# The low-part product of attention scores over 128 rows in place of 64

## The chip, the cores and the metric

One core of one Trainium2 chip. The metric is the device time of one execution in microseconds (us), the median of several runs. TensorE (PE) multiplies; its weight loads are listed apart as PEld. VectorE is DVE, ScalarE is ACT, GpSimd is POOL. SyncE (SP) issues nearly all DMAs, in the order of its queue.

## What is computed

Two layers of a decoder trunk over 1024 tokens of width 1024, in fp32. Layer 0 mixes tokens by two groups of attention heads behind one projection; layer 1 by a state-space recurrence and a short convolution. Each layer then has an MLP of width 4096 and a gated embedding. The change lies in layer 0's attention. Of the reference, the scores that it touches:

```python
sc = jnp.einsum('bqhcd,bkhcd->bhcqk', q_blk, kf) * scale      # dense heads, head width 64
sc = jnp.where(kpos[None, :] <= qpos[:, None], sc, -jnp.inf)
a = jax.nn.softmax(sc, axis=-1)
w = a[:, :, 0] - lam * a[:, :, 1]
```

The second group (a mixture of dilated windows) is computed as one masked softmax too, over the same kind of scores with another table of masks.

## The kernel before

**Exact operands in two parts.** An fp32 operand is split into a high part of type fp32r (`hi`, line 75, on ACT) and the low rest (`lo`, line 78, on DVE); a product is three matmuls, high by high, high by low and low by high (`mm3`, lines 93 to 95).

**The stage.** `attention` runs `at_start` and then `at_run`. `at_start` loads the eight blocks of x (line 1057), splits them, and makes q and k of pair 0. `at_run` goes through eight pairs of heads; a pair has two maps c = 0, 1 of head width 64, and the 1024 queries are taken in eight blocks of 128 (`qb`), two to a step. The score tile of one block has (qb + 1) x 128 columns, in pieces of at most 512.

**A score tile** (`emit_s`, line 1454) is two matmuls into one PSUM bank S of three. The contraction of a head is 64 long, so the tile of k that is read has k's high part in one half of the partitions and k's low part in the other, and the tile of q has q's high part twice. Line 1470 multiplies those over 128 rows: high by high plus high by low. Line 1471 adds q's low part by k's high part, over the 64 rows that hold them:

```python
nc.tensor.matmul(S, qk["q"][c][:, q], qk["k"][c][:, k], start=True, stop=False)
nc.tensor.matmul(S, qk["ql"][me, q], qk["k"][c][me, k], start=False, stop=True)
```

Then DVE adds the mask and takes the row minimum (line 1473), ACT takes the exponential (line 1478), and for the first four pairs DVE combines two maps (line 1492). Weights are transposed (line 1503), split, and multiplied with v (`pvu`, lines 93 to 95, 1527 and 1528).

**q and k** (`qk_out`, line 1154) are made half by half, 512 tokens each: DVE scales (`z`), ACT gives the high part (`zh`), DVE the low part. The pieces go to their places by DMAs of 64 rows on SP's queue (lines 1176 and 1177): four for a half of k, four for a half of q. q's low part needs no DMA, DVE writes it straight to the tile `ql`. `z`, `zh` and `zl` are tiles of one tag `z` of four buffers, which `ple_proj` (`ppo`) and `out_a` (`sq2`) use too. The tags `q0`, `q1`, `ql`, `k0`, `k1` have two buffers each, 1024 tokens wide; `at_start` borrows q's and k's for the blocks of x, and `ple_proj` for its operand.

**Order.** PE's order is set while the program is built: `at_run` weaves scores, transposes, products with v and filler (projections of the next pairs) by a model of costs. The other engines' orders come from the scheduler, SP's among them.

Of the kernel before, what the change touches and what calls it, by code (L numbers as in the profile page):

```python
# [7 lines left out]
F32 = mybir.dt.float32  # L8
F32R = mybir.dt.float32r
# [8 lines left out]
P = 128  # L18
T = 1024          # tokens
H = 512           # tokens of one matmul  # L20
D = 1024
KB = D // P       # 128-row blocks of the model width
FB = 32           # 128-row blocks of the MLP width
# [4 lines left out]
class Weave:  # L28
    """Order of TensorE's work: lanes of items that may start at a time, and filler for the waits."""
# [35 lines left out]
class Trunk:  # L65
# [40 lines left out]

    def rstd_split(self, acc, pool, width, tags, tags2=("z", "z", 4), bank=None):
        """(sum over partitions of acc / n_mean + eps) ** -0.5 on every partition, by the function returned."""
# [11 lines left out]
    def rstd_sum(self, accs, pool, width, tags, bank=None):  # L120
        """As rstd_split, of a sum of accs."""
        def sums(ps):
            for a in accs:
                self.nc.tensor.matmul(ps, self.ones.bitcast(F32), a, start=a is accs[0], stop=a is accs[-1])
        return self.rstd_of(sums, pool, width, tags, bank or self.bank)
# [22 lines left out]
    def xsplit(self, h, g, xp):  # L148
        """hi and lo of g * h, g per partition."""
# [74 lines left out]
    def chains(self, jobs, kbs):  # L224
        """jobs: (weights, operands, columns of the weights per block, half); the contraction outermost."""
# [12 lines left out]
    def blocks(self, src, xs, count, kbs, out, lead=2, split=None, pre=()):  # L238
        """Blocks m of W^T x: out(m, half, psum). The first ones take the contraction, or its two parts, outermost."""
# [24 lines left out]
    def stats_new(self, acc, sq):  # L264
        """Sums of squares; acc and sq are the (pool, tag, bufs) of their tiles."""
        return {"acc": None, "at": acc, "sq": sq}
# [11 lines left out]
    def rstd_full(self, st, rp, pool, n_z=4):  # L278
        """Inverse root mean square of each token, on every partition."""
# [91 lines left out]
    def ple(self, l, xs, st0, tp, xp):  # L371
# [3 lines left out]
        def out(m, n, ps):  # L375
# [13 lines left out]
            # tokens from (chunk, t) to (t, chunk)  # L389
# [10 lines left out]
    def ple_last(self, xs, st0, tp, wp):  # L400
# [4 lines left out]
        def final(hn, acc, s, n):  # L405
# [8 lines left out]
            if end:  # L414
                # with the gains applied before; few and large stores
# [69 lines left out]
    def pexp(self, out, x, tmp):  # L485
        """exp(x), to the last bits, 0 below the normal numbers."""
# [18 lines left out]
    def sincos(self, so, co, x, tmp):  # L505
# [18 lines left out]
        # the quadrant  # L524
# [22 lines left out]
    def s5_prep(self):  # L547
        """Matrices of the recurrence over chunks of 8 tokens, four groups at a time, to DRAM."""
# [3 lines left out]
        with tc.tile_pool(name="prep", bufs=1, side=LEFT, reuse_waits="tile") as pr:  # L552
# [23 lines left out]
            # powers 0..8 of the transition, and 7..0  # L576
# [22 lines left out]
            # (a - 1) / lambda  # L599
# [15 lines left out]
            # decay and rotation of one chunk  # L615
# [24 lines left out]
    def spill(self, pr, q, j, full):  # L640
        """hi and lo of a [128, 512] operand to DRAM."""
# [8 lines left out]
    def s5_quad(self, q, pr, pw, rv, cr, ci, rot, sgn, nsgn):  # L650
# [22 lines left out]
        def outer(out, tab, nt, X1, X2):  # L673
            """out[s, g, t, c] = tab0[s, t, g] X1[s, g, c] + tab1[s, t, g] X2[s, g, c]"""
# [15 lines left out]
        # rotation tables  # L690
# [42 lines left out]
    def recurrent(self, xp):  # L733
        tc, nc, A = self.tc, self.nc, self.A
        with tc.tile_pool(name="rc", bufs=1, side=RIGHT, reuse_waits="tile") as self.ap:
            gs, w = self.rc_run(xp)
            # the gate of the recurrence
# [19 lines left out]
    def rc_run(self, xp):  # L757
# [14 lines left out]
        # u, tokens on partitions, for two sets of 16 groups  # L772
# [52 lines left out]
        def conv(cb):  # L825
            """A block of channels of the gated convolution; tokens are (t, chunk)."""
# [26 lines left out]
            # the tokens before t = 0 are those of the chunk before  # L853
# [38 lines left out]
        def g_tiles(k):  # L892
            """Half of a block of the gate's operand, in the place of a quad's matrices."""
# [5 lines left out]
        def quad(q):  # L899
# [17 lines left out]
            def f_s():  # L917
# [16 lines left out]
                # back from the rotating frame, one chunk later  # L934
# [14 lines left out]
            def f_y():  # L949
# [4 lines left out]
                # by hi and lo of the matrices next to each other, summed on the way out  # L954
# [78 lines left out]
    def at_start(self, xp):  # L1033
        """hi and lo of the gained x, the first q and k as they come, and the inverse root mean squares."""
# [15 lines left out]
        for k in range(KB):  # L1050
            x = ap.tile([P, T], F32, name="x", tag=("q0", "q1", "k0", "k1")[k % 4], bufs=2)
# [47 lines left out]
    def ple_proj(self, l, m0, m1):  # L1099
        """(w_ple_proj^T p^T) of one layer, blocks m0 to m1, to DRAM; yields after each 128-row block of the contraction."""  # L1100
# [4 lines left out]
        for k in range(2):  # L1105
            raw = self.wp.tile([P, T], F32, tag="wr", bufs=2, name="praw")
            nc.sync.dma_start(raw, A["pT"][l, k])
            h, lo = [ap.tile([P, T], F32R, tag=t + str(k), bufs=2, name="ph") for t in "qk"]
            self.hi(h, raw)
            self.lo(lo, raw, h)  # L1110
            ps.append((h, lo))
        yield 0.0
        for m in ms:
# [3 lines left out]
            for n in range(2):  # L1117
                s = slice(n * H, (n + 1) * H)
                b = self.bank()
                for k in range(2):  # L1120
                    c = slice(k * 512 + (m % 4) * P, k * 512 + (m % 4) * P + P)
                    self.mm3(b, (ww[0][:, c], ww[1][:, c]), (ps[k][0][:, s], ps[k][1][:, s]), k == 0, k == 1)
# [30 lines left out]
    # projections: generators that yield after each 128-row block of a contraction  # L1153
    def qk_out(self, i, which, n, ps):
        nc, ap = self.nc, self.ap
        d = self.qkt.setdefault(i, {})
        if which not in d:
            d[which] = [ap.tile([P, T], F32R, name=f"{which}{c}", tag=f"{which}{c}", bufs=2) for c in range(2)]
            if which == "q":
                d["ql"] = ap.tile([P, T], F32R, name="ql", tag="ql", bufs=2)  # L1160
# [5 lines left out]
        if which == "q":  # L1166
            l = d["ql"][:, t]
        else:
            l = ap.tile([P, H], F32R, name="zl", tag="z", bufs=4)
# [3 lines left out]
        for c in range(2):  # L1173
            me, ot = slice(64 * c, 64 * c + 64), slice(64 - 64 * c, 128 - 64 * c)
            dst = d[which][c]
            nc.sync.dma_start(dst[me, t].bitcast(F32), h[me].bitcast(F32))
            nc.sync.dma_start(dst[ot, t].bitcast(F32), (h if which == "q" else l)[me].bitcast(F32))
# [504 lines left out]
```

## Time and profile before

| | |
|---|---|
| median of 3 runs | 2702.02 us (2697.83 to 2704.56) |
| span of the profiled execution | 2700.3 us |
| PE busy | 2669.5 us (99%) |
| DVE busy | 1545.3 us (57%) |
| ACT busy | 816.1 us (30%) |
| start of the first and of the last score product | 56.6 us and 609.2 us |

The page gives the profiled execution's span, from its first instruction to its last, and no time of its own beside that; the whole times of the three runs lie 2.5 us below to 4.3 us above it. Busy time of PE counts matmuls that overlap, with modelled ends; the start of one to the start of the next tells the pace. In a timeline a row gives start, duration, engine, line, operation, output and inputs, and the rows and columns of the array (64\*128 is 64 rows), and in brackets the idle time before it.

### The profile page before, as it was taken

The numbers are of one execution on the slowest core, as the hardware profiler recorded it, in microseconds if no ns is written. First come the engines' busy times: TensorE is split into PE (matmuls) and PEld (weight loads), VectorE is DVE, ScalarE is ACT, GpSimd is POOL, SyncE is SP. The second block draws the span as 40 slices with busy tenths as digits, with TensorE's granted clock in tenths as the row PEclk, the third lists the DMA queues.
The fourth block names the chain that finished last, engine by engine and source line by source line (L and its number), as shares of the span: only waits on it lengthen the run. The fifth ranks groups of instructions, "written<-read, shape, count | busy, mean of one in ns | idle before, by whom it ended". The sixth has DMA issues, their size and how long they took to land.

```text
span 2700.3 us, 32493 instructions
## 1 busy us (share of the span) xinstructions
PE 2669.5 (99%) x12680; PEld 2159.5 (80%) x12680; DVE 1545.3 (57%) x3083; ACT 816.1 (30%) x1337; POOL 71.3 (3%) x34
## 2 busy tenths in 40 slices
PE   8999999999999999999999999999999999999998
PEld 6778787878888888888888897888888888888887
DVE  6776655554675556456657768653543344334476
ACT  5444444553222111111224432332211111111244
POOL 1110101100000000000000000000000000000000
PEclk9999999999999999999999999999999999999999
DMA  4332412164111122122224655341111111111152
GB/s 160 102 90 73 124 47 75 49 213 176 50 65 62 61 82 83 61 69 83 82 85 159 222 174 172 123 157 46 47 47 47 48 48 46 48 50 48 63 190 94
DMA packets 120826, 251.06 MB, mean 93 GB/s; under 512 B 17632, under 2 KB 49632, under 8 KB 120672
## 3 DMA queue, kind: packets, MB, share of 16 engines
q1 hardware_dynamic: 120400, 248.72, 27.7%
q8 instruction: 100, 1.64, 0.2%
q14 instruction: 54, 0.44, 0.1%
q10 hardware_dynamic: 272, 0.26, 0.0%
HBM read 174.35 MB, written 56.62 MB: 86 GB/s over the span
## 4 chain that ended last, share of the span: by engine, by line
PE 93%; DVE 4%; ACT 1%; issue 1%; DMA 1%; SPq 0%; DVEq 0%; ACTq 0%
PE mm L93 28%; PE mm L95 27%; PE mm L94 27%; PE S L1471 2%; PE S L1470 2%; PE tp L1503 2%; PE o L1528 1%; PE o L1527 1%; PE S L1595 1%; PE o L94 0%; PE o L93 0%; PE o L95 0%; PE mm L717 0%; PE S L1545 0%; DMA x<-xT 0%
## 5 line engine op out<-in xcount | busy, mean ns | idle before, releaser
L93 PE MATMUL mm<-xh,wh 128*128 128x512 f32 (+1 forms) x2016 | 792.6, 393 | 0.0
L94 PE MATMUL mm<-xl,wh 128*128 128x512 f32 (+1 forms) x2016 | 782.6, 388 | 0.0
L95 PE MATMUL mm<-xh,wl 128*128 128x512 f32 (+1 forms) x2016 | 782.5, 388 | 0.0
L75 ACT ACTIVATE wh<-wr 128x1024 fp32r<-128x1024 f32 (+1 forms) x207 | 218.4, 1055 | 937.5 <-PE mm L94 895.5
L95 PEld LDWEIGHTS mm<-xh,wl 128*128 128x128 f32 x2016 | 379.2, 188 | 87.0
L93 PEld LDWEIGHTS mm<-xh,wh 128*128 128x128 f32 x2016 | 379.4, 188 | 86.1 <-issue 3.8
L94 PEld LDWEIGHTS mm<-xl,wh 128*128 128x128 f32 x2016 | 380.1, 189 | 81.1
L93 PE MATMUL mm<-hh,wh 128*128 128x512 f32 x1024 | 406.6, 397 | 0.0
L95 PE MATMUL mm<-hh,wl 128*128 128x512 f32 x1024 | 405.9, 396 | 0.0
L94 PE MATMUL mm<-hl,wh 128*128 128x512 f32 x1024 | 405.9, 396 | 0.0
L357 DVE TENSOR_TENSOR h<-mm,h 128x512 f32<-128x512 f32 x256 | 176.5, 690 | 293.3 <-PE mm L95 292.0
L336 DVE TENSOR_TENSOR z<-mm,rstd 128x512 f32<-128x512 f32 x128 | 88.0, 690 | 305.9 <-PE mm L95 305.9
L88 DVE TENSOR_TENSOR wl<-wr,wh 128x1024 fp32r<-128x1024 f32 x181 | 220.8, 1220 | 69.5 <-ACT wh L75 69.0
L93 PEld LDWEIGHTS mm<-hh,wh 128*128 128x128 f32 x1024 | 192.8, 188 | 48.2 <-issue 1.5
L95 PEld LDWEIGHTS mm<-hh,wl 128*128 128x128 f32 x1024 | 192.9, 188 | 47.0
L94 PEld LDWEIGHTS mm<-hl,wh 128*128 128x128 f32 x1024 | 192.9, 188 | 46.7
L75 ACT ACTIVATE hh<-z 128x512 fp32r<-128x512 f32 x128 | 80.9, 633 | 348.3 <-DVE z L337 345.4
L1478 ACT ACTIVATE p<-p,m 128x128 f32<-128x128 f32 (+7 forms) x128 | 99.0, 774 | 91.9 <-DVE m L1473 89.8
L93 PE MATMUL mm<-wh,xh 128*128 128x256 f32 x384 | 116.1, 302 | 2.2 <-DVE v L1226 1.5
L94 PE MATMUL mm<-wl,xh 128*128 128x256 f32 x384 | 110.3, 287 | 0.0
L95 PE MATMUL mm<-wh,xl 128*128 128x256 f32 x384 | 110.3, 287 | 0.0
L78 DVE TENSOR_TENSOR hl<-z,hh 128x512 fp32r<-128x512 f32 x128 | 87.6, 687 | 39.1 <-ACT hh L75 39.1
(377 smaller groups left out, 2937.5 us busy)
## 6 DMA issues: line engine op xcount, KB each, us to landing
wr<-w_m SPq DMA_DIRECT2D x128, 512.0 KB, 3.2
s<-s SPq DMA_DIRECT2D x64, 256.0 KB, 4.3
q<-zh SPq DMA_DIRECT2D x64, 128.0 KB, 2.4
pp<-ppo SPq DMA_DIRECT2D x32, 256.0 KB, 2.4
wr<-w_out SPq DMA_DIRECT2D x16, 512.0 KB, 3.2
hm<-h SPq DMA_DIRECT2D x16, 512.0 KB, 2.6
wr<-w_pg SPq DMA_DIRECT2D x16, 512.0 KB, 3.9
wr<-w_in SPq DMA_DIRECT2D x15, 512.0 KB, 3.4
```

What stands on the lines that cost most here:

```text
L75: self.nc.scalar.activation(out, in_, AF.Copy, scale=scale)
L78: self.nc.vector.tensor_tensor(out, full, hi.bitcast(F32), ALU.subtract)
L88: self.weng.tensor_tensor(l, raw, h.bitcast(F32), ALU.subtract)
L93: mm(ps, L[0], R[0], start=first, stop=False)
L94: mm(ps, L[0], R[1], start=False, stop=False)
L95: mm(ps, L[1], R[0], start=False, stop=last)
L336: nc.vector.tensor_tensor(z, ps, r[0][:, s], ALU.mult)
L357: nc.vector.tensor_tensor(h[m][:, s], ps, h[m][:, s], ALU.add)
L1470: nc.tensor.matmul(S, qk["q"][c][:, q], qk["k"][c][:, k], start=True, stop=False)
L1471: nc.tensor.matmul(S, qk["ql"][me, q], qk["k"][c][me, k], start=False, stop=True)
L1478: nc.scalar.activation(pt[:, :w], pt[:, :w], AF.Exp, bias=m, scale=-1.0, accum_out=den)
L1503: nc.tensor.transpose(tps[:, off + n * P : off + n * P + P], maps[j][:, kb * P : kb * P + P], self.ident)
```

## The change

The low part of q is laid out like its high part: twice, in both halves of the partitions. The second matmul then takes all 128 rows, and so adds q's low part by k's low part, which was left out before. q's tiles are made by halves of the tokens, `q0`, `q1`, `ql0` and `ql1` with three buffers of 512 tokens each in place of two of 1024 for `q0`, `q1` and `ql`. Each half of q has eight DMAs in place of four, and its low part passes through a tile of tag `z`. `at_start` takes the blocks of x from `k0`, `k1` and `p`, and `ple_proj` splits one of its two operand blocks by halves. The sums that `at_run` plans with are the same.

```diff
 def at_start(self, xp):
-            x = ap.tile([P, T], F32, name="x", tag=("q0", "q1", "k0", "k1")[k % 4], bufs=2)
+            x = ap.tile([P, T], F32, name="x", tag=("k0", "k1", "p")[k % 3], bufs=(2, 2, self.n_maps)[k % 3])
...
 def ple_proj(self, l, m0, m1):
-            h, lo = [ap.tile([P, T], F32R, tag=t + str(k), bufs=2, name="ph") for t in "qk"]
-            self.hi(h, raw)
-            self.lo(lo, raw, h)
-            ps.append((h, lo))
+            if k == 0:
+                whole = [ap.tile([P, T], F32R, tag=f"k{j}", bufs=2, name="ph") for j in range(2)]
+                halves = [[t[:, n * H : n * H + H] for t in whole] for n in range(2)]
+                self.hi(whole[0], raw)
+                self.lo(whole[1], raw, whole[0])
+            else:
+                halves = [[ap.tile([P, H], F32R, tag=f"{x}{j}", bufs=3, name="ph") for j in range(2)] for x in ("q", "ql")]
+                for n, (h, lo) in enumerate(halves):
+                    self.hi(h, raw[:, n * H : n * H + H])
+                    self.lo(lo, raw[:, n * H : n * H + H], h)
+            ps.append(halves)
...
 def qk_out(self, i, which, n, ps):
-        if which not in d:
-            d[which] = [ap.tile([P, T], F32R, name=f"{which}{c}", tag=f"{which}{c}", bufs=2) for c in range(2)]
-            if which == "q":
-                d["ql"] = ap.tile([P, T], F32R, name="ql", tag="ql", bufs=2)
...
-        if which == "q":
-            l = d["ql"][:, t]
-        else:
-            l = ap.tile([P, H], F32R, name="zl", tag="z", bufs=4)
+        l = ap.tile([P, H], F32R, name="zl", tag="z", bufs=4)
         self.lo(l, z, h)
...
-        for c in range(2):
+        if which == "k":
+            if n == 0:
+                d["k"] = [ap.tile([P, T], F32R, name=f"k{c}", tag=f"k{c}", bufs=2) for c in range(2)]
+            out = [(d["k"][c][:, t], h, l) for c in range(2)]
+        else:
+            for x in ("q", "ql"):
+                d[x, n] = [ap.tile([P, H], F32R, name=f"{x}{c}", tag=f"{x}{c}", bufs=3) for c in range(2)]
+            out = [(d[x, n][c], a, a) for x, a in (("q", h), ("ql", l)) for c in range(2)]
+        for j, (dst, a, b) in enumerate(out):
+            c = j % 2
             me, ot = slice(64 * c, 64 * c + 64), slice(64 - 64 * c, 128 - 64 * c)
-            dst = d[which][c]
-            nc.sync.dma_start(dst[me, t].bitcast(F32), h[me].bitcast(F32))
-            nc.sync.dma_start(dst[ot, t].bitcast(F32), (h if which == "q" else l)[me].bitcast(F32))
+            nc.sync.dma_start(dst[me].bitcast(F32), a[me].bitcast(F32))
+            nc.sync.dma_start(dst[ot].bitcast(F32), b[me].bitcast(F32))
...
 def emit_s(self, u, live):
-        q = slice(qb * P, qb * P + P)
-        me = slice(64 * c, 64 * c + 64)
+        q = slice(qb % 4 * P, qb % 4 * P + P)
+        qh, ql = [qk[x, qb // 4][c][:, q] for x in ("q", "ql")]
...
-            nc.tensor.matmul(S, qk["q"][c][:, q], qk["k"][c][:, k], start=True, stop=False)
-            nc.tensor.matmul(S, qk["ql"][me, q], qk["k"][c][me, k], start=False, stop=True)
+            nc.tensor.matmul(S, qh, qk["k"][c][:, k], start=True, stop=False)
+            nc.tensor.matmul(S, ql, qk["k"][c][:, k], start=False, stop=True)
```

**PE, the first scores of pair 0.** Names: S the score bank, k0 and q0 the tiles of map 0, k1 and q1 those of map 1. Before:

```order
L95 MATMUL mm_611<-wh_421,xl_214 128x256
L1470 MATMUL S_633<-k0_506,q0_518 128x128
L1471 MATMUL S_633<-k0_506,ql_520 128x128
L1470 MATMUL S_641<-k1_507,q1_519 128x128
L1471 MATMUL S_641<-k1_507,ql_520 128x128
L1470 MATMUL S_652<-k0_506,q0_518 128x256
```

Now:

```order
L95 MATMUL mm_626<-wh_421,xl_214 128x256
L1481 MATMUL S_648<-k0_512,q0_524 128x128
L1482 MATMUL S_648<-k0_512,ql0_526 128x128
L1481 MATMUL S_656<-k1_513,q1_525 128x128
L1482 MATMUL S_656<-k1_513,ql1_527 128x128
L1481 MATMUL S_667<-k0_512,q0_524 128x256
```

Nothing moved: PE's order is the same from the first instruction to the last, only the operand of each second product differs.

**SP, the first halves of q and k of pair 0.** zh and zl are the high and low part of a half as the engines leave them. Before:

```order
L1176 DMA q0_518<-zh_523 64x512
L1177 DMA q0_518<-zh_523 64x512
L1176 DMA q1_519<-zh_523 64x512
L1177 DMA q1_519<-zh_523 64x512
L1176 DMA k0_506<-zh_585 64x512
L1177 DMA k0_506<-zl_587 64x512
```

Now:

```order
L1187 DMA q0_524<-zh_520 64x512
L1188 DMA q0_524<-zh_520 64x512
L1187 DMA q1_525<-zh_520 64x512
L1188 DMA q1_525<-zh_520 64x512
L1187 DMA ql0_526<-zl_522 64x512
L1188 DMA ql0_526<-zl_522 64x512
L1187 DMA ql1_527<-zl_522 64x512
L1188 DMA ql1_527<-zl_522 64x512
L1187 DMA k0_512<-zh_591 64x512
L1188 DMA k0_512<-zl_593 64x512
```

Four DMAs of the low part stand behind the four of the high part, ahead of k's second half; so it is for each of the sixteen halves of q.

**SP, the loads at the start.** x is a block of the input, w_v the weights of the first v. Before:

```order
L1057 DMA x<-xT 128x1024
L208 DMA ident<-ident 128x128
L1057 DMA x<-xT 128x1024 x6
L1137 DMA lqk<-lqk 128x256
L1150 DMA sg<-sub_gain 128x1
L82 DMA wr<-w_v 128x1024 x2
```

Now:

```order
L1057 DMA x<-xT 128x1024
L208 DMA ident<-ident 128x128
L1057 DMA x<-xT 128x1024 x5
L1145 DMA lqk<-lqk 128x256
L1158 DMA sg<-sub_gain 128x1
L82 DMA wr<-w_v 128x1024 x2
L1057 DMA x<-xT 128x1024
```

One block of x, the sixth, is loaded behind both pieces of w_v.

## Rows read from the trace of the kernel before

**Rows 1.** The page: busy us (share of the span) xinstructions.

```profile
PE 2669.5 (99%) x12680; PEld 2159.5 (80%) x12680; DVE 1545.3 (57%) x3083; ACT 816.1 (30%) x1337; POOL 71.3 (3%) x34
```

**Rows 2.** Stretches, the scores' and the rest: length, busy, granted clock, DMA.

```profile
56.60:610.00 553.40, 548.52 (x2995) 431.93 (x2994) 344.01 (x927) 270.81 (x606) 55.92 (x23) 0.99 0.32 95
610.00:2700.30 2090.30, 2073.57 (x9455) 1689.76 (x9453) 1163.24 (x2111) 515.17 (x694) 3.81 (x3) 1.00 0.26 90
```

**Rows 3.** The two score lines: duration ns min/median/max, first and last start.

```profile
L1470 PE MATMUL S<-k,q x192: 219/392/794, 56.6 to 608.8; 128*128 128x512 f32 x96, 128*128 128x128 f32 x32, 128*128 128x256 f32 x32, 128*128 128x384 f32 x32
L1471 PE MATMUL S<-k,ql x192: 322/490/792, 56.8 to 609.2; 64*128 64x512 f32 x96, 64*128 64x128 f32 x32, 64*128 64x256 f32 x32, 64*128 64x384 f32 x32
```

**Rows 4.** Timeline of PE, two score tiles and what follows.

```profile
603.72 0.39 PE L1470 MATMUL S<-k,q 128*128 128x512 f32 x1
604.04 0.50 PE L1471 MATMUL S<-k,ql 64*128 64x512 f32 x1
604.47 0.45 PE L1470 MATMUL S<-k,q 128*128 128x384 f32 x1
604.84 0.44 PE L1471 MATMUL S<-k,ql 64*128 64x384 f32 x1
605.21 0.50 PE L93 MATMUL mm<-ph,wh 128*128 128x512 f32 x1
605.54 0.39 PE L94 MATMUL mm<-ph,wh 128*128 128x512 f32 x1
```

**Rows 5.** Timeline of PE's weight loads, the same place.

```profile
604.04 0.18 PEld L1471 LDWEIGHTS S<-k,ql 64*128 64x128 f32 x1 [0.25 <-issue]
605.21 0.19 PEld L93 LDWEIGHTS mm<-ph,wh 128*128 128x128 f32 x1 [0.18 <-issue]
605.31 0.19 PEld L94 LDWEIGHTS mm<-ph,wh 128*128 128x128 f32 x1
```

**Rows 6.** Timeline of PE, 128-row products behind each other.

```profile
601.52 0.40 PE L95 MATMUL mm<-ph,wl 128*128 128x512 f32 x1
601.75 0.40 PE L93 MATMUL mm<-ph,wh 128*128 128x512 f32 x1
...
602.68 0.28 PE L1527 MATMUL o<-th,v 128*128 128x256 f32 x1
602.80 0.28 PE L1528 MATMUL o<-tl,v 128*128 128x256 f32 x1
```

**Rows 7.** Timeline of PE, the first, narrowest score tiles.

```profile
56.79 0.32 PE L1471 MATMUL S<-k,ql 64*128 64x128 f32 x1
57.04 0.33 PE L1470 MATMUL S<-k,q 128*128 128x128 f32 x1
```

**Rows 8.** Waits of PE's loads, 56.6 to 610 us: us, times, longest.

```profile
PEld S L1471 <- issue: 35.3, 135, 0.4
...
PEld S L1470 <- DVE m L1473: 3.0, 6, 1.0
PEld tp L1503 <- DVE p L1492: 2.0, 2, 1.3
```

**Rows 9.** DVE's groups by shape, 56 to 610 us: busy us, mean ns.

```profile
L1473 DVE CUSTOM_DVE_ANT_0 p<-S,tab 128x512 f32<-128x512 f32 x80 | 54.9, 686 | 25.0 <-PE S L1471 24.5
L1473 DVE DVE_READ_ACCUMULATOR2_ANT m<- 128x1 f32 x191 | 15.7, 82 | 0.0
```

**Rows 10.** Timeline of SP, and the DMA table: KB each, us to landing.

```profile
48.33 0.60 SPq L1177 DMA_DIRECT2D q<-zh  x1
...
q<-zh SPq DMA_DIRECT2D x64, 128.0 KB, 2.4
x<-xT SPq DMA_DIRECT2D x7, 512.0 KB, 8.5
```

**Rows 11.** Waits of ACT and DVE for a DMA, 50 to 625 us.

```profile
ACT wh L75 <- DMA q<-zh: 4.0, 1, 4.0
DVE z L1163 <- DMA k<-zl: 3.5, 1, 3.5
```

**Rows 12.** Timeline of SP and of PE at the start.

```profile
12.04 0.33 SPq L82 DMA_DIRECT2D wr<-w_v  x1
...
25.23 0.50 PE L94 MATMUL S<-xl,wh 128*128 128x512 f32 x1 [0.45 <-DVE xl L1059]
```

**Rows 13.** A stretch of the scores, columns as in rows 2.

```profile
340.00:350.00 10.00, 9.99 (x57) 8.92 (x57) 4.76 (x17) 3.13 (x9) 0.00 (x0) 0.78 0.09 30
```

More of the change, by code (lines that the diff above doesn't have):

```diff
@@ L1121, in ple_proj @@
                     c = slice(k * 512 + (m % 4) * P, k * 512 + (m % 4) * P + P)
-                    self.mm3(b, (ww[0][:, c], ww[1][:, c]), (ps[k][0][:, s], ps[k][1][:, s]), k == 0, k == 1)
+                    self.mm3(b, (ww[0][:, c], ww[1][:, c]), ps[k][n], k == 0, k == 1)
                     if k == 0:
```

## The prediction

> **What bounds the kernel now.** I read the page's busy shares first. PE is busy 99% of the span, DVE 57%, ACT 30% [rows 1]: PE's own instructions are the path, unless something inside them is not work. The table of stretches places the change: all scores lie between 56.6 and 610 us, and there too PE is busy 548.5 of 553.4 us while DVE has 344.0 and ACT 270.8 [rows 2]. The 2090.3 us behind are PE's as well, so what PE gains among the scores reaches the end whole, as long as nothing else comes late. Next, the score lines by shape: 192 pairs of products, 96 of 512 columns and 32 each of 384, 256 and 128 [rows 3]. Their modelled durations hide their pace, so I go to the timeline and read start to start.
>
> There the reader is to see this. Products over 128 rows that follow each other start every 0.23 us at 512 columns (601.52 to 601.75) and every 0.12 us at 256 (602.68 to 602.80) [rows 6]. Two score tiles, of 512 and 384 columns, and the first product behind them take 1.82 us, from 603.72 to 605.54 [rows 4]. The loads say why: the load of the 64-row weights starts only at 604.04, with its matmul, and the load engine was idle 0.25 us before it; the first 128-row load behind the group starts at 605.21, again with its matmul, after 0.18 us idle; the next, at 605.31, is 128 rows behind 128 rows and starts 0.23 us ahead of its matmul at 605.54 [rows 4, 5]. So at each change between 128 and 64 rows PE neither streams nor preloads. 135 such waits of the 64-row loads alone are listed, for no reason that the profile shows [rows 8].
>
> **The change part by part.**
>
> *PE, the gain.* The group of rows 4 has three products of 512 columns and two of 384. At the pace of unbroken 128-row work that is 3 x 0.23 + 2 x 0.175 = 1.04 us; 0.175 is the middle between 0.23 and 0.12, which are 512 and 256 columns [rows 6]. The excess is 1.82 - 1.04 = 0.78 us for four changes of rows (in and out of each 64-row product): 0.195 us each. The change makes all rows 128 and keeps PE's order, so every pair loses both. For 160 pairs of 256 to 512 columns: 320 x 0.195 = 62.4 us. At 128 columns a change costs less: 57.04 - 56.79 = 0.25 us from a 64-row product to the next [rows 7]. A 128-row product of that width starts the next within 0.12 us, since 256 columns do [rows 6], so at least 0.13 us goes: 64 x 0.13 = 8.3 us. Together **70.7 us**. More columns or rows cost nothing themselves: the 64-row products of 512 columns stream no faster than the 128-row ones beside them [rows 4].
>
> [...]
>
> *Waits that the faster PE meets.* PE takes a 512-column tile in 2 x 0.23 = 0.46 us then, where in rows 4 it takes 0.75 (603.72 to 604.47). DVE needs 0.686 + 0.082 = 0.77 us for it [rows 9]. Within a group of tiles PE was as slow as DVE and will be faster; the three banks and the filler between groups must cover that. Today PE's loads wait 3.0 us for the row minimum, and 2.0 for the combination of maps [rows 8]. Late next will be just these, and the transposes behind them. Bounds: 0, if banks and filler cover all, and 0.77 - 0.46 = 0.31 us for each of the 96 wide tiles, 30 us, if they cover nothing. DVE's load in the stage only rises from 344 of 553 us to 344 of some 490, so I stay nearer to today's row and take **12 us**, more than double its 5.
>
> *SP, 64 more DMAs.* Sixteen halves of q have four more each; one takes SP 0.6 us and lands after 2.4 us [rows 10]. That is 38 us of SP's time, spread over 500 us on a queue that is waiting for ACT most of the time: nothing, as long as no bank waits. The tile of the low part, though, now holds a buffer of tag z until the last of eight DMAs has landed, 8 x 0.6 + 2.4 = 7.2 us, and ACT or DVE can stand behind such a buffer, as they did twice, for 4.0 and 3.5 us, PE hardly noticing [rows 11]. For the first pair: SP issued its eighth DMA at 48.33 [rows 10]; four more make 51.3, and the low part must first get its z buffer, when k's first DMAs have landed, so all lies some us later but still within about 54 us, ahead of the first score at 56.6 [rows 3]. I take 0 here, 0 to 5.
>
> *The start.* The sixth block of x stands behind both w_v loads, the first of which SP issued at 12.04 [rows 12]. With 8.5 us to landing [rows 10] it is there at about 22, then ACT and DVE split it, and PE wanted its low part at 25.23, already waiting 0.45 us for it [rows 12]. Bounds: below zero by that 0.45, if the constants' work that DVE now does earlier clears its way, and up 5 us, if w_v delays it by as much again as its own transfer. I take **2 us**, the side that the queue's order points to.
>
> *The rest.* DVE's low part of q is the same instruction on another tile. The three calls of `ple_proj` each split one block in two halves: three more instructions on ACT and on DVE, beside 209 and 283 us of idle time there [rows 2]. The half-wide third buffer of q needs PE's scores of the first four blocks of the pair before, which stand ahead of it by most of a pair. All nothing.
>
> The sum: 70.7 - 12 - 0 - 2 = **57 us**. Made on the profiled span of 2700.3 us that is 2643; the median of the runs lies 1.7 us above that span, so **2645 us** to be compared with 2702.0.
>
> [...]
>
> **The rivals.** 0.3%, or 8 us, is about what a measurement of this kernel can tell from no change.
>
> *DVE becomes the bound inside the groups.* For it: 0.77 against 0.46 us a tile. Against it: most groups are two tiles long, three banks stand ready, and DVE is idle 209 us in the stage [rows 2]. At its price of 30 us beside the 12: 2702 - (70.7 - 30 - 12 - 2) = **2675 us**. It decides where groups of more than three tiles follow each other without filler.
>
> *The z buffers stall ACT or DVE, and the kernel is slower.* The place is `qk_out` of pairs 1 to 7, 14 halves of q. If each blocks an engine for the full 7.2 us with PE waiting behind, that is 101 us against 70.7 - 14 = 57 us of gain: 2702 + 44 = **2746 us**. It turns slower from 57 / 14 = 4.1 us of PE's time per half. For it: four buffers and in-order engines. Against it: two waits of 4.0 and 3.5 us in 28 halves today [rows 11], at 4.8 us a half, and q's halves come one by one behind eight pieces of filler.
>
> [...]
>
> **How the numbers follow.** My forecast, 2645, gets 0.73: the price of a change of rows is read directly, and PE's order is untouched. DVE inside the groups 0.17, no effect 0.05, the z stall 0.05. Faster takes the first two, 0.90; no effect is the same, 0.05; the z stall slower, 0.05. The range's lower end is the gain with no new wait, no loss at the start, and the clock spared: 2702 - 70.7 - 4 = 2627, say 2628. Its upper end takes in the DVE rival, 2675, say 2676. The last two rivals stay out, with 0.10.
>
> **What would show it.** The second product's rows read 128\*128 and the issue waits before its loads are gone; 512-column score products start 0.23 us apart; the last score product starts near 552 us in place of 609; what follows has its length of 2090 us. [...] I am wrong in the main step if the last score moves by less than 25 us.

## The result, and the profile after

The changed kernel takes 2656.3 us (median of 4 runs, 2655.02 to 2657.36) against 2699.93 us for the kernel before in the same comparison: a ratio of 0.9829, with an interval of 0.9815 to 0.9844, or 43.6 us less. The forecast was 2645 us, within 2628 to 2676. The profiled execution took 2655.4 us in all.

The page of the changed kernel, its span and its busy times (columns as in [rows 1]):

```profile
span 2653.6 us, 32638 instructions
PE 2605.4 (98%) x12680; PEld 2154.6 (81%) x12680; DVE 1546.6 (58%) x3086; ACT 814.0 (31%) x1340; POOL 72.5 (3%) x34
```

The span fell by 46.7 us, and PE lost 64 us of busy time, DVE and ACT next to nothing. The stretches, to be held against [rows 2]:

```profile
58.00:565.00 507.00, 487.54 (x3029) 431.64 (x3028) 349.39 (x936) 271.04 (x613) 56.82 (x23) 0.99 0.43 122
565.00:2653.60 2088.60, 2071.22 (x9438) 1687.26 (x9435) 1160.68 (x2106) 513.56 (x692) 3.81 (x3) 1.00 0.27 90
```

The gain lies among the scores: PE idles 19.5 us there where it idled 4.9 before, and still the stretch is some 46 us shorter. The rest keeps its length. The group of tiles of [rows 4] now reads, in the timeline of PE:

```profile
557.48 0.40 PE L1481 MATMUL S<-k,q 128*128 128x512 f32 x1
557.72 0.39 PE L1482 MATMUL S<-k,ql 128*128 128x512 f32 x1
557.95 0.34 PE L1481 MATMUL S<-k,q 128*128 128x384 f32 x1
558.12 0.34 PE L1482 MATMUL S<-k,ql 128*128 128x384 f32 x1
558.30 0.39 PE L93 MATMUL mm<-ph,wh 128*128 128x512 f32 x1
558.52 0.39 PE L94 MATMUL mm<-ph,wh 128*128 128x512 f32 x1
```

From 557.48 to 558.52 are 1.04 us, where it was 1.82: the number that the prediction worked out for this group. The loads there, then the waits of PE's loads and of PE from 56 to 570 us (us, times, longest):

```profile
557.72 0.19 PEld L1481 LDWEIGHTS S<-k,q 128*128 128x128 f32 x1
557.95 0.19 PEld L1482 LDWEIGHTS S<-k,ql 128*128 128x128 f32 x1
```

```profile
PEld S L1482 <- issue: 0.7, 2, 0.5
```

```profile
PE S L1482 <- DMA ql<-zl: 4.1, 4, 1.9
PE tp L1514 <- DVE p L1503: 3.9, 4, 1.4
PE S L1481 <- DVE m L1484: 3.4, 4, 1.4
...
PE S L1481 <- DMA q<-zh: 1.0, 1, 1.0
```

Each load starts with the matmul ahead of its own, 0.23 us early. The 135 issue waits of 35.3 us [rows 8] are two of 0.7 us. New are 5.2 us of waits for DMAs (the rows are rounded), above all for q's low part.

By parts, in the two profiled executions: the first score starts 3.3 us later (56.6 to 59.9); from there to the first product of the last tile it takes 501.5 us in place of 552.2, 50.7 less; from there to the end 0.7 more. Between the two PE idles 14.6 us more: 9.1 for DVE (4.9 to 14.0, summed over the timeline), 5.2 for DMAs, and 0.3 in gaps too short to be listed. So the products themselves gave 50.7 + 14.6 = 65.3 us.

### The profile page after: what moved, and what is told of

It is laid out like the page before. It is cut to its first block, busy times and chain, and to the rows that moved or that the text cites. A ratio compares the mean times of both kernels' runs of the same rounds, so it can differ in the third digit from the quotient of the medians.

```text
span 2653.6 us, 32638 instructions
## 1 busy us (share of the span) xinstructions
PE 2605.4 (98%) x12680; PEld 2154.6 (81%) x12680; DVE 1546.6 (58%) x3086; ACT 814.0 (31%) x1340; POOL 72.5 (3%) x34
## 4 chain that ended last, share of the span: by engine, by line
PE 90%; DVE 5%; ACT 1%; DMA 1%; issue 1%; SPq 0%; DVEq 0%; ACTq 0%
PE mm L93 27%; PE mm L95 27%; PE mm L94 27%; PE tp L1514 2%; PE S L1481 1%; PE S L1482 1%; PE o L1539 1%; PE o L1538 1%; PE S L1606 1%; DVE zl L78 1%; DVE p L1484 0%; DMA pp<-pp 0%; DVE p L1503 0%; DVE tl L78 0%; PE mm L717 0%
## 5 line engine op out<-in xcount | busy, mean ns | idle before, releaser
L94 PEld LDWEIGHTS mm<-hl,wh 128*128 128x128 f32 x1024 | 192.9, 188 | 46.7
```

The source lines that it names most:

```text
L94: mm(ps, L[0], R[1], start=False, stop=False)
```

## The experiments

All times are medians of four runs; ratios are to the kernel before, run on the same chip in the same comparison. There were five comparisons (the change; e1 to e5; e6 and e7; e8 to e10; e11 and e12), and the kernel before took 2699.9, 2704.2, 2703.4, 2702.7 and 2704.6 us in them. So a few us between rows of different comparisons need the profiles' support beside the times. In the diffs, ... stands for lines left out.

| run | edit, in short | us | ratio (interval) |
|---|---|---|---|
| the change | | 2656.3 | 0.9829 (0.9815 to 0.9844) |
| e1_rows64 | change, 64 rows again | 2721.7 | 1.0070 (1.0053 to 1.0086) |
| e2_old128 | before, 128 rows | 2642.9 | 0.9777 (0.9761 to 0.9793) |
| e4_grouped | before, products grouped | 2682.0 | 0.9919 (0.9902 to 0.9936) |
| e5_start | change, x ahead of w_v | 2649.8 | 0.9806 (0.9787 to 0.9826) |
| e6_zero | e5, low part without DMAs | 2666.0 | 0.9853 (0.9837 to 0.9870) |
| e7_actq | e5, low part's DMAs from ACT | 2660.6 | 0.9837 (0.9822 to 0.9852) |
| e8_pool4 | e5, POOL's work in four pieces | 2641.0 | 0.9777 (0.9760 to 0.9793) |
| e9_wldve | e5, POOL's work on DVE | 2643.1 | 0.9782 (0.9768 to 0.9797) |
| e10_dma4 | e2, four more DMAs ahead of q's | 2655.3 | 0.9829 (0.9815 to 0.9844) |
| e11_act6 | e8, six DMAs for a half of q | 2636.4 | 0.9743 (0.9727 to 0.9760) |
| e12_act4 | e8, four DMAs for a half of q | 2643.8 | 0.9772 (0.9757 to 0.9786) |

The clock's loss below is (1 - granted clock) x 10 us, summed over the 10-us stretches from 60 to 640 us: 6.8 us in the kernel before and 6.8 in the change.

**e1: the new tiles and DMAs, the second product on 64 rows** (low by low is left out again, as in the kernel before).

```diff
+        me = slice(64 * c, 64 * c + 64)
...
-            nc.tensor.matmul(S, ql, qk["k"][c][:, k], start=False, stop=True)
+            nc.tensor.matmul(S, ql[me], qk["k"][c][me, k], start=False, stop=True)
```

> The changed kernel with its new tiles, halves and DMAs, but with the second product over the 64 rows of q's low part by k's high part, as before. Theory (the gain is the changes between 128 and 64 rows; the new tiles cost the late start of 3.3 us and, where PE is quick enough to meet them, the low part's DMAs): all the gain goes, 2700 + 3 to 5 = 2703 to 2705 us. Rival A (the new tiles and DMAs cost nothing, all that was given back are waits for DVE): 2700 us. Rival B (part of the gain came from the halves, say from earlier loads): clearly below 2700.

The direction is right, the size is not: 65.4 us above the change, but 2721.7 where 2703 to 2705 was expected. That 65.4 is the gain of the rows again is in part chance: among the scores e1 is 70.2 us longer than the change, with 11.9 us more lost to the clock and 7.0 us less idle time of PE, which leaves 65.3 for the products. Against the kernel before the span is 20.8 us longer: 2.7 at the start, 4.3 of waits for DMAs, 3.1 more for DVE, 11.9 of clock, less 1.2 behind the last score. 8.5 of the 18.7 us that the clock loses in e1 lie in two stretches (columns as in [rows 2]) that hold or follow a wait of 2.83 us for q and one of 1.35 us for its low part; 5 more follow a wait of 1.11 us for DVE at 279.75:

```profile
580.00:590.00 10.00, 8.41 (x19) 5.04 (x19) 3.02 (x13) 3.86 (x12) 0.00 (x0) 0.52 0.87 216
590.00:600.00 10.00, 10.00 (x31) 6.97 (x31) 5.55 (x16) 3.64 (x10) 0.00 (x0) 0.63 0.19 57
```

So the new layout has a price of its own, apart from the rows; how much of the clock's loss belongs to it was not tried.

**e2: the rows alone.** The kernel before, with all 128 rows of its own tile `ql`. That tile holds the other map's low part in its other half, so this run adds that by k's low part in place of q's own.

```diff
-            nc.tensor.matmul(S, qk["ql"][me, q], qk["k"][c][me, k], start=False, stop=True)
+            nc.tensor.matmul(S, qk["ql"][:, q], qk["k"][c][:, k], start=False, stop=True)
```

> The kernel before with its tiles and DMAs, only the second product taken over all 128 rows of its one tile of low parts (the other map's low part by k's low part is added, a term that the reference does not have, of the size of rounding). No DMA more, no late load at the start. Theory: 67 us of changes go, 9 of DVE waits come: 2700 - 58 = 2642, 2639 to 2647. Rival A: the same as the changed kernel, 2656, since DVE's waits are all that was given back there.

2642.9 us: the theory's time. All engines have the order of before, so 61.3 us are the rows' alone, with 11.1 us more of waits for DVE among the scores (16.0 in place of 4.9) paid, 5.0 us less lost to the clock, and no wait for a DMA. The change is 13.4 us slower than this. Between the profiles (14.4 us) that is the start 2.9, waits for DMAs 5.2, the clock 5.0 (1.8 lost here, 6.8 there) and 1.7 behind the last score; waits for DVE and ACT among the scores are 2.2 longer in e2, and 1.8 stay unplaced.

**e4: 64 rows kept, fewer changes.** Where a tile has two pieces, both first products stand ahead of both second ones.

```diff
...
+        for S, k in zip(Ss, ks):
             nc.tensor.matmul(S, qk["q"][c][:, q], qk["k"][c][:, k], start=True, stop=False)
+        for S, k in zip(Ss, ks):
             nc.tensor.matmul(S, qk["ql"][me, q], qk["k"][c][me, k], start=False, stop=True)
+        for S, k in zip(Ss, ks):
...
```

> The kernel before, 64-row second products kept, but in the 64 score tiles wider than 512 columns the two first products come ahead of the two second ones, so that 64 rows follow 64 rows: two changes of rows in place of four. Theory (the change costs, 0.195 us each): 128 changes fewer, 25 us, less some 3 to 8 us because DVE gets the first bank later: 2678 to 2683. Rival C (every 64-row product costs for itself, because it is 64 rows): 2700 or a little slower.

2682.0 us, as expected. The timeline of PE, five products of 512 columns (the first two rows hold two each):

```profile
581.51 0.57 PE L1470 MATMUL S<-k,q 128*128 128x512 f32 x2
582.01 0.68 PE L1472 MATMUL S<-k,ql 64*128 64x512 f32 x2
582.62 0.50 PE L93 MATMUL mm<-ph,wh 128*128 128x512 f32 x1
582.95 0.39 PE L94 MATMUL mm<-ph,wh 128*128 128x512 f32 x1
```

From 581.51 to 582.95 are 1.44 us, 0.28 more than five times 0.232, for two changes. 64 tiles lose two changes of rows each. The span is 23.9 us shorter with 1.6 us more of waits for DVE and the same loss to the clock, so a change costs 25.5 / 128 = 0.20 us; by the medians of the runs, 22.2 us apart, it is 0.19. The prediction had 0.195. What costs is the change of rows, not the 64 rows. (DVE, ACT and SP got another order in places; the waits count it.)

**e5: the start put right.** The third and sixth block of x are loaded in two halves into buffers of q, so SP loads all of x ahead of w_v again.

```diff
-            x = ap.tile([P, T], F32, name="x", tag=("k0", "k1", "p")[k % 3], bufs=(2, 2, self.n_maps)[k % 3])
+            if k % 3 == 2:
+                xp2 = [ap.tile([P, H], F32, name="x", tag=f"q{k // 3}", bufs=3) for _ in range(2)]
...
```

> The changed kernel, with the third and sixth block of x in two halves in q's tiles, so that SP issues all of x ahead of w_v again. Theory: the 3.3 us at the start come back, 2653, first score product near 56.6 us. Rival A: 2656, the start was hidden by what follows.

6.5 us less than the change, more than expected; the first score starts at 56.0 us, 3.9 earlier, and the stretch behind the last score is 2.9 us shorter. Of these, 2.4 are the clock's, which loses 5.0 us there in e5 and 7.4 in the change. The waits for DMAs stay (5.1 us): they are another matter. In the change the start had read, in the timelines of SP and PE (products of the third, sixth and eighth block of x):

```profile
15.18 0.91 SPq L82 DMA_DIRECT2D wr<-w_v  x2
17.81 0.33 SPq L1057 DMA_DIRECT2D x<-xT  x1
...
17.80 0.50 PE L94 MATMUL S<-xl,wh 128*128 128x512 f32 x1 [0.67 <-DVE xl L1059]
...
27.57 0.50 PE L94 MATMUL S<-xl,wh 128*128 128x512 f32 x1 [0.52 <-DVE xl L1059]
...
35.38 0.50 PE L94 MATMUL S<-xl,wh 128*128 128x512 f32 x1 [1.39 <-DVE xl L1059]
```

In the kernel before, the same products start at 16.20, 25.23 and 32.01 us. So PE is 1.6 us late at the third block already, before the sixth is wanted. Half of that comes from the first block, whose second half lands at 8.00 us in place of 7.26; the rest from the third itself, which lands at 15.25 in place of 11.96, since SP loads the fourth and fifth ahead of it in the change. At the sixth block PE is 2.3 us late, at the eighth 3.4. e5 moves the third and the sixth together and does not tell them apart.

**e6 and e7: two ways around the low part's DMAs, both worse.** e6 leaves low by low out, as the kernel before did: DVE writes the low part into the map's own half, and POOL zeroes the other (first diff). e7 lets ACT issue the low part's DMAs (second).

```diff
+                nc.gpsimd.memset(d["ql", n][c][ot].bitcast(F32), 0.0)
+                self.lo(d["ql", n][c][me], z[me], h[me])
...
```

```diff
+            dma = nc.scalar.dma_start if which == "q" and j >= 2 else nc.sync.dma_start
...
```

> Edit: as e5_start, but the low part of q is not passed through a buffer and four DMAs; DVE writes it straight into the map's own half of its tile (two instructions on 64 partitions in place of one on 128), and GpSimd sets the other half to zero. The second product still takes 128 rows. Theory: what is left of the new layout's cost in e5_start is the waits of PE for the low part and the last of q's DMAs, 5.1 us in five waits, and the clock that falls behind them, about 3 us more than in e2_old128. With SP's queue at four DMAs for a half of q again, the waits should be below 1 us in all and the time 2650 - 8 = 2642 us, 2639 to 2645; DVE's 16 to 32 more instructions are hidden. Rival A: the waits stem from q's turn in the program (the projection ends late against the first scores of the pair), not from the number of DMAs: then q's high part is waited for as now, 2649 to 2651 us. Rival B: DVE's added work or the zeroing stands ahead of the row minimum or the scaling in DVE's order: PE's waits for DVE grow by over 5 us, 2650 us or more.

> Edit: as e5_start, but the four DMAs of q's low part in each half are issued by ACT in place of SP; the same DMAs, the same bytes. Theory (SP's queue issues eight one behind another at 0.6 us, the low parts last): the low parts start about 2.4 us earlier and the five waits for DMAs, 5.1 us in e5_start, shrink to below 2 us; time 2650 - 3 to 8 = 2642 to 2647 us. Rival A: the transfers or the bytes are what is late, not the queue's turn: the waits stay, 2649 to 2651 us. Rival B: ACT stands behind a DMA that waits for DVE's low part, the exponentials come late and PE waits for them or for transposes: DMA waits go but PE's waits for ACT and DVE grow by as much or more, 2650 to 2658 us.

Rows of PE's waits, first of e6, then of e7:

```profile
PE S L1493 <- DVE m L1496: 8.6, 4, 2.8
...
PE S L1493 <- DMA q<-zh: 2.0, 1, 2.0
```

```profile
PE tp L1521 <- ACT p L1496: 5.3, 5, 2.3
...
PE S L1489 <- DMA ql<-zl: 3.2, 3, 1.3
PE S L1488 <- DMA q<-zh: 2.1, 2, 1.1
```

e6: waits for DMAs fall from 5.1 to 2.0 us, but its rival B came: 6.4 us more of waits for DVE among the scores, 2.2 for ACT, a start 2.9 later, and the clock loses 15.3 us where e5 loses 5.1: 18.6 us by these parts, and the span is 19.1 longer than e5's (2.0 more lie behind the last score, so the parts overlap a little). The wait of 2.0 us that is left is one, for q's high part at pair 7, though only four DMAs make a half of q here. e7: its rival B, and rival A too: the waits for DMAs stay (5.8 us) and 6.0 us for ACT come on top; it lost 10.9 us to e5. Both edits also shift the scheduler's order on ACT and DVE, so their size isn't one mechanism's.

**e8 and e9: what holds DVE.** Around the late scores of the last pair, the change's timeline reads:

```profile
508.81 2.40 POOL L88 TENSOR_TENSOR wl<-wr,wh 128x1024 fp32r<-128x1024 f32 x1 [16.41 <-ACT wh L75]
509.28 0.47 SPq L1187 DMA_DIRECT2D k<-zh  x1
509.28 2.48 DVE L78 TENSOR_TENSOR zl<-z,zh 128x512 fp32r<-128x512 f32 x1 [0.73 <-ACT zh L75]
511.79 0.46 SPq L1188 DMA_DIRECT2D k<-zl  x1
...
513.64 0.52 SPq L82 DMA_DIRECT2D wr<-w_out  x1
514.21 0.44 SPq L290 DMA_DIRECT2D xh<-y0h  x1
514.92 0.47 SPq L1187 DMA_DIRECT2D q<-zh  x1
...
520.81 0.30 PE L1481 MATMUL S<-k,q 128*128 128x128 f32 x1 [1.05 <-DMA q<-zh]
...
523.03 0.44 PE L1482 MATMUL S<-k,ql 128*128 128x128 f32 x1 [1.93 <-DMA ql<-zl]
```

DVE's low part takes 2.48 us, 0.69 elsewhere, and ends 0.55 us behind POOL's instruction (511.76 and 511.21). Ten of the 30 low parts of q and k from 56 us on read like this. SP stands behind this one with k's low part. The theory put q's DMAs behind it too, but the trace does not: DVE had been idle 1.72 us, for PE's projection, when it scaled q at 513.48, and q's first DMA goes out when ACT has made the high part (514.26 to 514.90).

So e8 splits POOL's subtraction (first diff), and e9 gives it to DVE (second).

```diff
-        self.weng.tensor_tensor(l, raw, h.bitcast(F32), ALU.subtract)
+        n = 4 if self.weng is self.nc.gpsimd else 1
+        for c in range(n):
+            s = slice(c * 1024 // n, (c + 1) * 1024 // n)
+            self.weng.tensor_tensor(l[:, s], raw[:, s], h[:, s].bitcast(F32), ALU.subtract)
```

```diff
-            self.weng = nc.gpsimd
+            self.weng = nc.vector
```

> Edit: as e5_start, but GpSimd makes the low part of each weight tile during the scores in four pieces of 256 columns in place of one of 1024; same data. Theory: in all traces a DVE instruction that runs when such a piece of 2.4 us is under way ends 0.55 us behind the piece's end (ten low parts of q and k took 1.8 to 2.9 us in place of 0.69 us in e5_start); before q's last half this holds k's low part, so SP's queue and q's DMAs, by about 1.8 us. With pieces of about 0.6 us the hold is below 0.6 us each; PE's waits for DVE (15.6 us) and for DMAs (5.1 us) shrink together by 4 to 8 us: 2642 to 2646 us. Rival A: the next piece takes its turn ahead of DVE, which is held as long as before: 2648 to 2652 us, long low parts remain. Rival B: four starts in place of one make the weights' low part late, PE waits for POOL: over 2652 us.

> Edit: as e5_start, but during the scores DVE makes the low part of each weight tile, 23 instructions of 1.3 us, in place of GpSimd. Theory as in e8_pool4: DVE gets 30 us of work and loses about 27 us of being held, so its busy time hardly changes, but no row of a low part over 0.7 us is left; PE's waits for DVE and DMAs fall by 3 to 8 us: 2642 to 2647 us. Rival: the 1.3 us stand in DVE's order ahead of row minima, which is as bad as being held: 2648 to 2655 us.

Both came out faster than e5: e8 by 8.8 us (7.8 in the span), a little below its range, e9 by 6.7. In e8 every other engine has e5's order throughout the scores. DVE's low parts (busy us, mean ns), first in e5, then in e8:

```profile
L78 DVE TENSOR_TENSOR zl<-z,zh 128x512 fp32r<-128x512 f32 x30 | 38.0, 1266 | 7.8 <-ACT zh L75 7.6
```

```profile
L78 DVE TENSOR_TENSOR zl<-z,zh 128x512 fp32r<-128x512 f32 x30 | 22.9, 762 | 7.6 <-ACT zh L75 6.7 <-DMA q<-zh 0.8
```

And PE's waits for DMAs in e8:

```profile
PE S L1491 <- DMA ql<-zl: 3.5, 4, 1.5
PE S L1490 <- DMA q<-zh: 2.0, 1, 2.0
```

PE's waits for DVE fall from 15.6 to 8.5 us: this part of the theory holds. Those for DMAs do not fall (5.1 to 5.6 us): that part is wrong, q is late without POOL's help. At pair 7, where 3.5 of the 5.6 us lie, its high part lands some 6 us after its issue (the section on the prediction says why).

**e10: four more DMAs alone.** e2 with four copies of q's high part to a scratch tensor ahead of q's own four DMAs.

```diff
...
+        if which == "q":
+            for c in range(2):
+                for r in (slice(0, 64), slice(64, 128)):
+                    nc.sync.dma_start(self.du_d[2 * i + n][c][r], h[r].bitcast(F32))
...
```

> Edit: as e2_old128 (the layout of before, second product over 128 rows), plus four DMAs of 64 rows for each half of q that copy its high part to a scratch tensor in DRAM, on SP's queue ahead of q's own four; nothing reads them. This doubles the number alone, without the low part's path. Theory (eight DMAs in a row delay the last one by 4 x 0.6 = 2.4 us, and that is what the new layout costs at the starts of pairs): PE waits for q's DMAs of 3 to 8 us in all appear, with clock drops behind them: 2647 to 2654 us. Rival: the number of DMAs is not what makes q late (the path through a low part that GpSimd delays is): 2641 to 2645 us, no wait for DMAs over 0.5 us.

12.4 us above e2, just over the range. Waits for q's DMAs appear where e2 had none:

```profile
PE S L1475 <- DMA q<-zh: 3.3, 5, 0.8
```

In the span, 14.3 us longer, 8.1 lie in and ahead of the scores: 3.3 for these waits, 2.5 more for DVE, 0.7 at the start, and 1.6 that stay unplaced; the clock loses 1.7 us among the scores as in e2. The other 6.2 lie behind the last score, 3.4 of them the clock's, with one wait of 3.62 us for DVE; the scheduler had put ACT and DVE in another order there, and in places among the scores. So the number of DMAs alone makes q late. Its price here is the 3.3 us of waits, at pairs 2, 3 and 5; pair 7 waits for no DMA. The rest of the loss is not shown to be theirs.

**e11 and e12: fewer DMAs in the changed layout.** ACT makes the copy that stays in its own 64 partitions, in e11 of the high part (j below 2, as shown), in e12 of both (without that bound).

```diff
...
+            if which == "q" and j < 2:
+                self.nc.scalar.activation(dst[me], a[me].bitcast(F32), AF.Copy)
+            else:
                 nc.sync.dma_start(dst[me].bitcast(F32), a[me].bitcast(F32))
```

> Edit: as e8_pool4, but of the two copies of q's high part of each map the one that stays in its own 64 partitions is made by ACT (two instructions of 64x512 for each half of q); six DMAs for a half of q in place of eight. Theory: eight issues in a row on SP's queue make q late at pairs 3 and 7, 5.6 us of waits in e8_pool4 with about 2 us of clock behind them; two issues less let the rest land 1.2 us earlier, so about half of it goes: 2637 to 2640 us. Rival A: ACT's 1.2 us more for each half stand ahead of exponentials or of the next high part, PE's waits for ACT and DVE grow as much: 2640 to 2648 us. Rival B: what is late is the transfer, not the issue (the DMA engines are full of weights then): 2640 to 2642 us.

> Edit: as e11_act6, and ACT also copies q's low part in its own 64 partitions: four instructions of ACT and four DMAs for a half of q, as many DMAs as in the kernel before. Theory: all waits for q's and ql's DMAs fall to about 1 us, with the clock behind them: 2633 to 2638 us. Rival A: ACT's copies of the low part wait for DVE and hold the exponentials behind them, as in e7_actq, where PE's waits for ACT were 6.0 us: 2642 to 2650 us. Rival B: as in e11_act6, 2640 to 2642 us.

e11 is the fastest kernel of the study, 2636.4 us, slightly below its range and 19.9 below the change; its interval and e8's only just touch. Its waits for DMAs, to be held against those of e8:

```profile
PE S L1493 <- DMA q<-zh: 1.7, 1, 1.7
PE S L1494 <- DMA ql<-zl: 1.3, 3, 0.9
```

The waits for DMAs halve (5.6 to 2.9 us), and the clock loses 1.7 us in place of 3.4. At pairs 3 and 5 they all but go (2.1 to 0.2 us), as the theory had it. At pair 7 rival B holds: 2.8 of 3.5 us stay, and q's high part lands 6.2 us after its issue. In e12 they fall on to 0.8 us, but its rival A came: waits for ACT rise from 0.2 to 3.4 us, those for DVE from 7.6 to 10.9.

## Why the prediction was right, and where it was not

**The main step held.** The mechanism is the change of rows, shown from three sides: with the orders unchanged the rows alone give 61.3 us (e2), taking them back costs 65.4 (e1), and removing 128 of the changes with 64 rows kept gives 0.19 to 0.20 us each (e4). With PE's idle time and the clock's loss taken out, the traces agree more closely than the times: from the first score to the last PE needs 540.9 us in the kernel before, 540.7 in e1, 516.5 in e4, 475.5 in the change and 473.8 in e2. The signs of the mechanism came: rows 128\*128, the issue waits gone but for two, 0.23 us from start to start, and what follows has its length (2091.1 and 2091.9 us). The last score product starts at 561.7 us, not near 552: it moved by 47.5 us, well over the 25 that would have spoken against the step, and the missing 10 are accounted for below. By the prediction's own measure of 8 us the kernel is faster, by 1.7%.

No effect, to which the prediction gave 0.05, is out: the full-row load at 557.72 runs behind a full-row matmul, starts 0.23 us ahead of its own and delays nothing, and of 135 issue waits with 35.3 us two with 0.7 us are left.

**Gross gain: 70.7 us forecast, 65.3 measured.** By the medians of start to start, a pair of 512-column products went from 0.38 + 0.425 to 0.24 + 0.23 us, which is 0.335 us and not 0.39: the change into the 64-row product costs less there (0.14 us) than the one out of it. Over 96 pairs that is 5.3 us. The price had been averaged over one group of rows 4. At 128 columns 0.335 us went per pair, above the 0.26 that was taken as a lower bound, and 2.4 us in all; the 256-column pairs gave 0.03 less. These medians add up to 66.9 us; 1.6 of the 5.4 us that are missing stay unplaced.

**Waits for DVE: 12 us forecast, 9.1 measured,** and 11.1 in e2. The figure was a choice between bounds, and that it landed near is in part luck. What it missed is why DVE is late: about half of PE's waits for DVE go once POOL's work comes in pieces (15.6 us in e5, 8.5 in e8). Rows that showed it stood in the trace of before too, where seven low parts took 1.9 to 2.9 us. The first rival, DVE as the bound inside the groups, did not come; tiles of 512 columns start 0.24 and 0.23 us apart.

**The DMAs: this step failed.** The prediction costed 64 more DMAs at nothing because SP has time on average. PE waited 5.2 us for them at the first scores of pairs 3, 5 and 7, for two reasons. The first is the number. SP issues a half of q one DMA after another, and the low part last; at pair 3 in the change's timeline of SP:

```profile
247.56 0.60 SPq L1188 DMA_DIRECT2D q<-zh  x1
...
251.41 0.59 SPq L1188 DMA_DIRECT2D ql<-zl  x1
```

It is there about 2.3 us later, and PE wanted it 0.94 us earlier than it came, at 253.95. The mean over 500 us said nothing of the eight issues in a row just ahead of a deadline. This made the 2.2 us of pairs 3 and 5; e11, with two DMAs fewer, has next to nothing left of them.

The second reason, which joins the first in the 3.0 us of pair 7, is what stands ahead of q. The high part's four DMAs come first there, and still PE waits 1.05 us for them. DMAs of q's high part there, KB each and us to landing, in the change and in e2:

```profile
q<-zh SPq DMA_DIRECT2D x4, 128.0 KB, 5.2
```

```profile
q<-zh SPq DMA_DIRECT2D x4, 128.0 KB, 3.2
```

In the change two loads of 512 KB, of w_out and y0h, are issued at 513.64 and 514.21 us, just ahead of q's four. In the kernel before, e2, e4 and e10 no load of w_out stands there, only one of y0l (and e10's own four copies); the four DMAs land 2.3 to 3.5 us after their issue, and pair 7 waits for none of them. In the eight other runs with the two loads ahead, e6 with its four DMAs among them, the first two DMAs of q there take 5.0 to 6.6 us to land, and PE waits for q or its low part. Why the scheduler moved these loads, and what the wait is without them, was not tried.

The stretches with a lower clock moved there too: 0.83, 0.83 and 0.66 at 250, 390 and 520 us. The second rival, ACT or DVE held by the buffers of tag z, did not come: no wait of DVE for zl's DMAs is listed among the scores, and ACT's longest for a DMA is 4.0 us, as before [rows 11].

**The start: 2 us forecast, 3.3 measured,** inside its bounds, but only in part for the reason given, the sixth block behind w_v: 1.6 us were lost by the third block, half of them since its load stands behind those of the fourth and fifth, an order that the prediction did not look at (e5 takes the whole back). **The clock**: no run shows the 4 us that the range takes for it at its lower end. At 340 to 350 us of the kernel before it lost (1 - 0.78) x 10 = 2.2 us [rows 13]; from 60 to 640 us it lost 6.8 us in the change as before, in other places. (The idle times of 209 and 283 us that the prediction names for ACT and DVE stand the wrong way round; nothing hangs on it.)

Sum: 5.4 less gain, 2.9 less for DVE, 5.2 for DMAs, 0.3 in short gaps, 1.3 at the start and 0.7 behind the scores make the 10.0 us by which the span's gain fell short (46.7 of 56.7).

## What to carry to other kernels

On a PE-bound stretch, look in the weight loads for issue waits at changes of rows: filling the unused rows cost PE no time here (512-column products over 128 rows started 0.24 and 0.23 us apart) and gave 0.14 to 0.20 us per change. Cost the copies that this needs by the last issue ahead of the deadline and by the large loads that stand ahead of them in the queue, not by the queue's mean; with two of eight DMAs replaced by copies on ACT the kernel was 4.6 us faster (e11 against e8), with four 2.8 us slower. With the faster PE, DVE instructions that ended behind POOL's became waits of PE; POOL's work in smaller pieces took PE's waits for DVE from 15.6 to 8.5 us (e8 against e5).

## What the runs showed of the hardware

**DVE's low parts of q and k, with both operands in SBUF, ended some 0.55 us behind a POOL subtraction that they started under; subtractions with an operand in PSUM took their usual time.** Two rows of DVE in the change, under POOL's instruction from 236.66 to 239.06 us:

```profile
237.15 0.69 DVE L78 TENSOR_TENSOR tl<-tp,th 128x512 fp32r<-128x512 f32 x1 [0.83 <-ACT th L75]
237.75 1.85 DVE L78 TENSOR_TENSOR zl<-z,zh 128x512 fp32r<-128x512 f32 x1
```

The first reads the transposes `tp` from PSUM and takes its usual 0.69 us; so do all nine of its kind that start under POOL among the scores (0.68 to 0.69 us at 512 columns, 0.55 at 384). The second reads `z` and `zh` from SBUF and ends 0.54 us behind POOL, as do, with 0.53 to 0.55 us, all ten low parts of q and k that start under POOL in the change, and, with 0.54 to 0.56 us, all seven in the kernel before. The expectation of e8 says this of any DVE instruction; the traces show it for these low parts. Another subtraction of two SBUF operands, `ph` at 112.67 us in the change, started 0.08 us behind POOL's and took its usual 0.68 us, while POOL's took 3.01 us, where most take 2.4. With POOL's work in pieces of 256 columns (e8) the low parts of q and k take 0.76 us in the mean, 1.27 in e5.

**The granted clock was low behind some short waits of PE, and not behind others.** In e1 it was 0.52 and 0.63 of full speed at 580 to 590 and 590 to 600 us, with 4.2 us of waits for DMAs close together; in the change it was 0.66 at 520 to 530 us (0.50 from 524 to 528), with 3.0 us of them. In e10, waits of 0.83 and 0.80 us at 178 and 252 us were followed by no lower clock: 1.00 at 170 to 200 and at 250 to 280 us. What decides it was not tried.
